# The dt columns of an input projection: from split operands on the whole array to unsplit operands in four column blocks

## The chip, the cores and the metric

The kernel runs on one core of one Trainium2 chip. The metric is the device time of one launch in microseconds (us), the median of several runs; lower is better. The profile is of a single execution on the same core. Its engines are TensorE (PE for matrix products, PEld for loading the stationary operand), VectorE (DVE), ScalarE (ACT), GpSimd (POOL) and SyncE (SP, which here only issues DMAs).

## What is computed

One step of a hybrid decoder layer for 320 tokens (256 of a prompt, 64 = 8 x 8 of a batch of samples), model width 2048, all in float32. Cut to what matters here:

```python
h = rms_norm(x, p["norm_mix_pre"])
proj = h @ p["w_in"]                       # 2048 x 9248
a_u, a_v, z, xbc, dt_raw = ...             # columns 0, 2048, 4096, 6144, 9216:9248
gate_out = chunk_spatial_gate(a_u, a_v, ...)
xbc = silu(causal_depthwise_conv(xbc, ...))
dt = softplus(dt_raw + dt_bias)            # 32 heads
y, new_state = ssd_scan(xs, dt, -exp(a_log), bm, cm, state)
x = x + rms_norm(concat(gate_out, gated_norm(y)) @ p["w_out"])
x = x + rms_norm(conv_ffn(rms_norm(x), ...))
```

The change concerns `dt_raw`: the last 32 columns of the input projection, one for each SSD head, for all 320 tokens.

## The kernel before

**Layout.** Activations stand with features on partitions: x is 16 tiles of 128 features by 320 tokens. The input norm is split in two: `x_ready` (L539 on) multiplies each tile by its norm weight (`pre`, 16 columns) and splits the product into a high part `h_hi` and a remainder `h_lo`, both of the type fp32r. The reciprocal root `r1` of the mean square, a number for each token, is made later (`with_r1`) and multiplied onto the results of a projection when they leave PSUM.

**A projection** (`project`, L154 on) streams weights in slabs of 512 KB through three buffers: SP loads `wraw`, ACT casts it to `whi` (L119), DVE makes the remainder `wlo` (L121). A block of 128 x 128 weights then costs three products of 128 x 320 (`accumulate`, L130 to L132: hi by hi, hi by lo, lo by hi). A slab has eight such blocks, 24 products. Four PSUM buffers (pool `mm`) hold the four output tiles of a projection, so the next one waits for a buffer until its evacuation is done. A second PSUM pool, `ms`, has four buffers for small things (`misc`).

**Order.** First v (`v_pass` 0 to 3), then B and C of the SSD part (`conv_proj`), then dt, then the first group of SSD heads (`heads_in(0)`), then u, the gate's product and the rest. A list of generators, `bg`, holds background work: `tick` advances its first generator by one step, and `project` ticks after most slabs. The Tile framework's scheduler places each instruction in its engine's queue by priority; each engine then runs its queue in order.

**The first 64 us.** `flat` is a view of the tile `vt`, which is later filled with v: until then it holds `pre` and the unnormalised x (`xf`). `with_r1` sits in `bg`: it waits seven ticks, sums the squares, runs three Newton steps on DVE (L230 to L236), then transposes the result over the partitions (`spread`, L272), copies it to `r1` (ACT, L274) and issues the DMAs of `params` (L328 on). `turned(0)` writes the first part of v into `vt` after the second `v_pass`.

**dt before** (`steps`, L421 on): two slabs of 8 x 128 columns are loaded, the last 128 columns of `w_in`, of which the last 32 are dt's. They go through the same cast, remainder and 48 products as any other (tile `ps_dt`, a buffer of `mm`); rows 96 to 127 of the result are used. DVE multiplies by `r1` (L430, tile `dtf`), POOL repeats the sample columns (L431, L433), and later five transposes (L438, tile `dt_ps`) bring dt to tokens on partitions. From there come the softplus, the cumulated sums and the decays.

Of the kernel before, what the change touches and what calls it, by code (L numbers as in the profile page):

```python
# [9 lines left out]
F32 = mybir.dt.float32  # L10
# [3 lines left out]
ALU = mybir.AluOpType  # L14
# [3 lines left out]
P = 128  # L18
NP = 256
NB, TS = 8, 8  # L20
NS = NB * TS
NT = NP + NS
D = 2048
KD = D // P
DFF = 5632
NF = DFF // P
NH = 32
# [3 lines left out]
U0, V0, Z0, X0, B0, C0, DT0 = 0, 2048, 4096, 6144, 8192, 8704, 9216  # L31
# [3 lines left out]
def hybrid_step(  # L35
# [10 lines left out]
    act, dve, pool, pe, sp = nc.scalar, nc.vector, nc.gpsimd, nc.tensor, nc.sync  # L46

    w_in, w_out, ffn_w_up, ffn_w_down = w_in[0], w_out[0], ffn_w_up[0], ffn_w_down[0]
# [5 lines left out]
    mm = ctx.enter_context(tc.tile_pool(name="mm", bufs=4, space=PSUM))  # L54
    ms = ctx.enter_context(tc.tile_pool(name="ms", bufs=4, space=PSUM))

    def misc(name):
        return ms.tile([P, 512], F32, tag="ms", name=name)


    ident = cp.tile([P, P], F32, name="ident")
# [3 lines left out]
    with tc.high_priority(offset=300000):  # L65
        dve.memset(ones, 1.0)

        ps = misc("early")
# [10 lines left out]
    def masks():  # L79
        make_upper_triangular(nc, upper, 1.0, diag=True)  # L80
        make_lower_triangular(nc, later, 1.0, diag=False)
        make_block_diagonal(nc, bd2, TS)

        for r in range(4):
            rs = slice(32 * r, 32 * r + 32)
            pool.tensor_copy(bsel[rs], bd2[rs, rs].rearrange("p (b t) -> p b t", b=4)[:, :, 0])
        for r in range(2):
            rs = slice(64 * r, 64 * r + 64)
            dve.tensor_tensor(out=upper_s[rs], in0=upper[rs, rs], in1=bd2[rs, rs], op=ALU.mult)
        pool.memset(cmask, 1.0)  # L90
        cm4 = cmask.rearrange("p (h b) i -> p h b i", h=2)
        pool.affine_select(out=cm4, in_=cm4, pattern=[[0, 2], [-8, 4], [1, 32]],
                           compare_op=ALU.is_ge, fill=0.0, base=0, channel_multiplier=0)
        pool.affine_select(out=cm4, in_=cm4, pattern=[[0, 2], [8, 4], [-1, 32]],
                           compare_op=ALU.is_ge, fill=0.0, base=7, channel_multiplier=0)
# [8 lines left out]
    def first():  # L104

        return tc.high_priority(offset=200000)
# [5 lines left out]
    def slab(src):  # L112
        n = src.shape[2]
        with tc.high_priority(offset=100000):
            m = n * src.shape[1]
            raw = first_raw.pop(0) if first_raw else wp.tile([P, 1024], F32, tag="wraw", name="wraw", bufs=3)
            slab_load.append(sp.dma_start(raw[:, :m].rearrange("p (a n) -> p a n", n=n), src).ins)
            hi = wp.tile([P, 1024], F32R, tag="whi", name="whi", bufs=3)
            act.copy(hi[:, :m], raw[:, :m])  # L119
            lo = wp.tile([P, 1024], F32R, tag="wlo", name="wlo", bufs=3)  # L120
            dve.tensor_tensor(out=lo[:, :m], in0=raw[:, :m], in1=hi[:, :m].bitcast(F32), op=ALU.subtract)  # L121

        def block(k, c):
            o = k * n + c * P
            return hi[:, o:o + P], lo[:, o:o + P]
        return block

    def accumulate(ps, w, xhi, xlo, first, last):
        whi, wlo = w
        pe.matmul(ps, whi, xhi, start=first, stop=False)  # L130
        pe.matmul(ps, whi, xlo, start=False, stop=False)  # L131
        return pe.matmul(ps, wlo, xhi, start=False, stop=last).ins  # L132

    def rows_of(w, k0, nk, c0, n):
        return w[k0 * P:(k0 + nk) * P, c0:c0 + n].rearrange("(k p) n -> p k n", p=P)

    hT = [None, None]


    bg = []  # L140
# [84 lines left out]
    def rsqrt_of(ss, scale, n, rows=P):  # L225

        v = tp.tile([P, n], F32, tag=f"rs_v{n}", name="rs_v")[:rows]
        r = tp.tile([P, n], F32, tag=f"rs_r{n}", name="rs_r", bufs=3)[:rows]
        t = tp.tile([P, n], F32, tag=f"rs_t{n}", name="rs_t")[:rows]
        dve.tensor_scalar(out=v, in0=ss, scalar1=scale, scalar2=EPS, op0=ALU.mult, op1=ALU.add)  # L230
        dve.tensor_scalar(out=r.bitcast(I32), in0=v.bitcast(I32), scalar1=-0.5, scalar2=float(0x5F3759DF),
                          op0=ALU.mult, op1=ALU.add)
        for _ in range(3):
            dve.scalar_tensor_tensor(out=t, in0=v, scalar=-0.5, in1=r, op0=ALU.mult, op1=ALU.mult)
            dve.tensor_tensor(out=t, in0=t, in1=r, op=ALU.mult)
            ins = dve.scalar_tensor_tensor(out=r, in0=t, scalar=1.5, in1=r, op0=ALU.add, op1=ALU.mult).ins  # L236
        rsqrt_ins.append(ins)
        return r
# [20 lines left out]
    def token_sums(sq, ps=None, more=False):  # L259

        begins = ps is None
        ps = misc("tsum") if begins else ps
        for c, o in enumerate((0, P, NT - P)):
            ins = pe.matmul(ps[:, c:c + 1], sq[:, o:o + P], ones[:, 0:1], start=begins and c == 0, stop=not more and c == 2).ins  # L264
        sums_ins.append(ins)
        return ps if more else ps[:, 0:3]

    def spread(r, out=None):

        ps = misc("spread")  # L270
        for c, o in ((2, NT - P), (0, 0), (1, P)):
            spread_ins.append(pe.transpose(ps[:, o:o + P], r[:, c:c + 1].to_broadcast([P, P]), ident).ins)  # L272
        if out is not None:
            act.copy(out, ps[:, :NT])  # L274
        return ps[:, :NT]
# [43 lines left out]
    r1 = hp.tile([P, NT], F32, name="r1")  # L319
# [51 lines left out]
    with ExitStack() as mctx:  # L371
        op = mctx.enter_context(tc.tile_pool(name="op", bufs=1))
# [3 lines left out]
        LP = 347  # L376
# [41 lines left out]
        dec = op.tile([P, 5, NH], F32, name="dec")  # L418
        ed = op.tile([P, 4, 4], F32, name="ed")

        def steps():  # L421

            ps_dt = mm.tile([P, 512], F32, tag="mm", name="ps_dt")
            for s in range(2):
                wb = slab(rows_of(w_in, 8 * s, 8, DT0 - 96, P))
                for k in range(8):
                    kt = 8 * s + k
                    accumulate(ps_dt[:, :NT], wb(k, 0), hT[0][:, kt, :], hT[1][:, kt, :], kt == 0, kt == KD - 1)
            dtf = op.tile([P, NT + NS + 2 * P], F32, tag="dtf", name="dtf", bufs=1)
            dve.tensor_tensor(out=dtf[96:, :NT], in0=ps_dt[96:, :NT], in1=r1[96:], op=ALU.mult)  # L430
            pool.tensor_copy(dtf[96:, NT:NT + NS], dtf[96:, NP:NT])  # L431
            for i in range(2):
                pool.tensor_copy(dtf[96:, (3 + i) * P:(4 + i) * P].rearrange("p (q t) -> p q t", q=4),  # L433
                                 dtf[96:, NP + 32 * i:NP + 32 * i + 32].unsqueeze(1).to_broadcast([32, 4, 32]))
            yield
            ps = misc("dt_ps")
            for c in range(5):
                pe.transpose(ps[:, NH * c:NH * c + NH], dtf[96:, P * c:P * c + P], ident[96:, 96:])  # L438
            H5 = 5 * NH
            dve.tensor_tensor(out=dt, in0=ps[:, :H5].rearrange("p (c h) -> p c h", c=5),  # L440
                              in1=bias_bc.unsqueeze(1).to_broadcast([P, 5, NH]), op=ALU.add)

            e = op.tile([P, 5, NH], F32, name="sp_e")
            q = dec
# [22 lines left out]
            ps = misc("cs_ps")  # L467
# [15 lines left out]
            ps = misc("csT_ps")  # L483
# [12 lines left out]
            ps = misc("dec_ps")  # L496
# [4 lines left out]
            for r in range(2):  # L501
                rs = slice(32 * r, 32 * r + 32)
                pool.tensor_tensor(out=later_s[:, r], in0=later[:NS, rs].unsqueeze(1).to_broadcast([NS, 4, 32]),
                                   in1=bd[:, rs].unsqueeze(1).to_broadcast([NS, 4, 32]), op=ALU.mult)
                pe.matmul(ps[:, (3 + r) * NH:(4 + r) * NH], later_s[:, r].rearrange("p q t -> p (q t)"), da[:NS, 2],
                          start=True, stop=True)
# [10 lines left out]
        with tc.tile_pool(name="gp", bufs=1) as gp:  # L517
# [4 lines left out]
            pre = flat[:, :KD]  # L522
            xf = flat[:, KD:KD + KD * NT].rearrange("p (k n) -> p k n", n=NT)
            masks()

            wS = gp.tile([P, 4, NB, TS], F32, name="wS")
            pool.memset(wS[NS:], 0.0)
# [38 lines left out]
            def with_r1():  # L566
                yield from repeat(None, 7)
                with first():
                    dve.tensor_tensor(out=acc[:, 0, :], in0=acc[:, 0, :], in1=acc[:, 1, :], op=ALU.add)
                    r = rsqrt_of(token_sums(acc[:, 0, :]), 1.0 / D, 3)  # L570
                yield
                spread(r, r1)
                params()
                yield

            after_v = []

# [96 lines left out]
                    if j % 2:  # L674
                        yield

            spare_pads = op.tile([P, 4, NT], F32, tag="xs", name="xs_pads", bufs=2).rearrange("p k n -> p (k n)")
            spare_pads = [spare_pads[:, LP * i:LP * i + LP] for i in range(3)]
            normed = layer_norm()
            bg.append(normed)  # L680
            conv_proj(B0, 16, lambda j: bT[:, j, :], 50000)
            behind(bT[:, 0, 0:1])
            conv_proj(C0, 20, lambda j: cT[:, j, :], 50000)
            tasks = steps()
            next(tasks)
            bg.append(tasks)
            x0 = heads_in(0)
            finish(normed)
            uf = gate_up(0)
# [12 lines left out]
        with tc.tile_pool(name="sd", bufs=1) as sd:  # L702
# [8 lines left out]
            for c in range(4):  # L711
                ps = misc("bt_ps")
# [185 lines left out]
            tasks = [ssd(g) for g in range(4)]  # L898
# [114 lines left out]
    with tc.tile_pool(name="fp", bufs=1) as fp:  # L1013
# [190 lines left out]
        for ks in [slice(k, k + 2) for k in range(0, 10, 2)] + [slice(10, 11)]:  # L1204
            f = acc[:, ks, :]
            n = ks.stop - ks.start
# [5 lines left out]
        for ks in (slice(11, 12), slice(12, 14), slice(14, 16)):  # L1212
            f = acc[:, ks, :]
            n = ks.stop - ks.start
# [87 lines left out]
```

## Time and profile before

| | us |
|---|---|
| median of 3 runs | 1789.76 (1789.74 to 1791.35) |
| the profiled execution, its own time | 1790.97 |
| span of that execution, first to last instruction | 1789.3 |

The granted TensorE clock in the profile is 0.998 of full speed. In the timelines below, the columns are start in us, duration in us, engine, line, operation, output and inputs, partitions by columns of the stationary operand, shape of what is written or streamed, number of merged instructions, and in brackets the engine's idle time before it with what ended it. A matrix product's shown duration includes the time until its last result is out; products overlap, so what one costs the array is the distance from its start to the next start. In views of groups, the two numbers after the bar are busy us and the mean of one in ns. An fp32 product stands in the trace as two instructions (64 calls at L812 give 128 records), an fp32r product as one.

### The profile page before, as it was taken

The numbers are of one execution on the slowest core, as the hardware profiler recorded it, in microseconds if no ns is written. First come the engines' busy times: TensorE is split into PE (matmuls) and PEld (weight loads), VectorE is DVE, ScalarE is ACT, GpSimd is POOL, SyncE is SP. The second block draws the span as 40 slices with busy tenths as digits, with TensorE's granted clock in tenths as the row PEclk, the third lists the DMA queues.
The fourth block names the chain that finished last, engine by engine and source line by source line (L and its number), as shares of the span: only waits on it lengthen the run. The fifth ranks groups of instructions, "written<-read, shape, count | busy, mean of one in ns | idle before, by whom it ended". The sixth has DMA issues, their size and how long they took to land.

```text
span 1789.3 us, 31254 instructions
## 1 busy us (share of the span) xinstructions
PE 1775.5 (99%) x12241; PEld 1744.7 (98%) x12241; DVE 1191.2 (67%) x2058; ACT 794.3 (44%) x1101; POOL 276.6 (15%) x591
## 2 busy tenths in 40 slices
PE   9999999999999999999999999999999999999998
PEld 9999999999999898999999999999999999999997
DVE  7448664557867778577866675767666575656565
ACT  6343455333535364445645434443434343433334
POOL 2003200000210111002322212121101020101004
PEclk9999999999999999999999999999999999999999
DMA  7455544445664644454565656566554444444442
GB/s 246 144 165 165 189 148 153 153 153 179 226 198 147 201 154 151 142 170 153 161 196 191 206 181 202 182 197 206 183 185 154 153 147 153 156 149 149 154 156 95
DMA packets 228082, 303.83 MB, mean 170 GB/s; under 512 B 17408, under 2 KB 149856, under 8 KB 227744
## 3 DMA queue, kind: packets, MB, share of 16 engines
q1 hardware_dynamic: 216288, 281.89, 49.4%
q10 hardware_dynamic: 10160, 15.47, 2.4%
q0 software_dynamic: 1488, 4.49, 0.8%
q8 instruction: 96, 1.57, 0.4%
q14 instruction: 50, 0.41, 0.1%
HBM read 284.23 MB, written 17.58 MB: 169 GB/s over the span
## 4 chain that ended last, share of the span: by engine, by line
PE 92%; DVE 4%; DMA 1%; issue 1%; ACT 1%; POOL 0%; SPq 0%; DVEq 0%; ACTq 0%; POOLq 0%
PE ps L130 19%; PE ps L132 19%; PE ps L131 19%; PE pd L130 10%; PE pd L132 10%; PE pd L131 10%; DVE wlo L121 1%; PE y_ps L859 1%; PE yo_ps L812 1%; PE tsum L264 0%; PE sg L663 0%; PE up_ps L1152 0%; DMA wraw<-in_w_in 0%; DVE acc_mix L998 0%; PE xt_ps L360 0%
## 5 line engine op out<-in xcount | busy, mean ns | idle before, releaser
L121 DVE TENSOR_TENSOR wlo<-wraw,whi 128x1024 fp32r<-128x1024 f32 x472 | 588.7, 1248 | 385.3 <-ACT whi L119 382.6
L119 ACT CAST whi<-wraw 128x1024 fp32r<-128x1024 f32 x472 | 494.2, 1047 | 726.1 <-PE ps L131 430.7
L130 PE MATMUL ps<-h_hi,whi 128*128 128x320 f32 x2528 | 784.5, 311 | 2.8 <-DVE dtf L430 2.1
L131 PE MATMUL ps<-h_lo,whi 128*128 128x320 f32 x2528 | 780.4, 309 | 0.0
L132 PE MATMUL ps<-h_hi,wlo 128*128 128x320 f32 x2528 | 779.4, 309 | 0.5 <-DVE wlo L121 0.2
L130 PEld LDWEIGHTS ps<-h_hi,whi 128*128 128x128 f32 x2528 | 474.6, 188 | 8.4 <-issue 3.8
L131 PEld LDWEIGHTS ps<-h_lo,whi 128*128 128x128 f32 x2528 | 474.8, 188 | 1.5 <-issue 0.5
L132 PEld LDWEIGHTS ps<-h_hi,wlo 128*128 128x128 f32 x2528 | 474.1, 188 | 2.0 <-DVE wlo L121 1.8
L130 PE MATMUL pd<-fhi,whi 128*128 128x320 f32 x704 | 217.3, 309 | 0.0
L132 PE MATMUL pd<-fhi,wlo 128*128 128x320 f32 x704 | 217.3, 309 | 0.0
L131 PE MATMUL pd<-flo,whi 128*128 128x320 f32 x704 | 217.3, 309 | 0.0
L130 PE MATMUL pd<-ohi,whi 128*128 128x320 f32 x448 | 140.8, 314 | 0.0
L131 PE MATMUL pd<-olo,whi 128*128 128x320 f32 x448 | 139.2, 311 | 0.0
L132 PE MATMUL pd<-ohi,wlo 128*128 128x320 f32 x448 | 138.9, 310 | 0.0
L131 PEld LDWEIGHTS pd<-flo,whi 128*128 128x128 f32 x704 | 132.2, 188 | 0.7
L132 PEld LDWEIGHTS pd<-fhi,wlo 128*128 128x128 f32 x704 | 132.2, 188 | 0.0
L130 PEld LDWEIGHTS pd<-fhi,whi 128*128 128x128 f32 x704 | 132.2, 188 | 0.0
L216 DVE TENSOR_TENSOR acc_ffn<-acc_ffn,pd 128x320 f32<-128x320 f32 x160 | 77.5, 484 | 35.8 <-PE pd L132 34.8
L130 PEld LDWEIGHTS pd<-ohi,whi 128*128 128x128 f32 x448 | 84.1, 188 | 4.0 <-issue 2.5
L132 PEld LDWEIGHTS pd<-ohi,wlo 128*128 128x128 f32 x448 | 84.1, 188 | 0.6 <-issue 0.6
L131 PEld LDWEIGHTS pd<-olo,whi 128*128 128x128 f32 x448 | 84.2, 188 | 0.2 <-issue 0.2
L1049 POOL COPY ptf<-pad 128x2 f32<-128x2 f32 x88 | 20.8, 238 | 406.5 <-DVE pad L1037 406.0
(297 smaller groups left out, 1588.1 us busy)
## 6 DMA issues: line engine op xcount, KB each, us to landing
wraw<-in_ffn_w_up SPq DMA_DIRECT2D x176, 512.0 KB, 3.5
wraw<-in_w_in SPq DMA_DIRECT2D x144, 512.0 KB, 3.5
wraw<-in_ffn_w_down SPq DMA_DIRECT2D x88, 512.0 KB, 3.3
wraw<-in_w_out SPq DMA_DIRECT2D x64, 512.0 KB, 3.3
st<-in_state_ssm SPq DMA_DIRECT2D x64, 256.0 KB, 3.8
out_ssm_state_sample<-st ACTq DMA_DIRECT2D x32, 256.0 KB, 2.7
cs<-dacs_d SPq DMA_DIRECT2D x16, 320.0 KB, 3.5
xr<-in_xT SPq DMA_DIRECT2D x4, 640.0 KB, 4.6
```

Source lines behind the costliest of these rows:

```text
L119: act.copy(hi[:, :m], raw[:, :m])
L121: dve.tensor_tensor(out=lo[:, :m], in0=raw[:, :m], in1=hi[:, :m].bitcast(F32), op=ALU.subtract)
L130: pe.matmul(ps, whi, xhi, start=first, stop=False)
L131: pe.matmul(ps, whi, xlo, start=False, stop=False)
L132: return pe.matmul(ps, wlo, xhi, start=False, stop=last).ins
L216: dve.tensor_tensor(out=acc[:, nb, :], in0=acc[:, nb, :], in1=ps[:, :NT], op=ALU.add)
L812: pe.matmul(ps_yo[row:row + 32, :256], cms[:, 4 * h + i, :], st[h][:, 256 * r:256 * r + 256], start=i == 0, stop=i == 3, tile_position=(0, ...
L859: pe.matmul(ps[64 * i:64 * i + 64, cols], w(hl), x(hl, m, cpx), tile_position=(0, 64 * i), **flags)
L1049: pool.tensor_copy(ptf[:, k, :], pad[:, 256:258])
```

## The change

- dt's products leave `steps`. A new generator `dt_columns`, started in `with_r1` behind `params()`, loads the 32 columns alone into the tile `dt_w` (128 x 16 x 32, 256 KB in runs of 128 bytes) on SP's queue. POOL multiplies them by `pre`.
- Seven ticks later, 16 fp32 products of 128 x 32 weights by 128 x 320 of the unsplit `xf` follow. Feature tiles 4i to 4i+3 go to the column blocks 0, 32, 64 and 96 of the array, and so to four quarters of the partitions of one PSUM tile (`dt_four`, a `misc` buffer): each quarter sums four of the 16 feature tiles.
- DVE evacuates all four quarters in one instruction with `r1`; POOL's three copies now cover 128 partitions.
- The five transposes become five fp32 products with `heads4`, a 128 x 32 matrix with four ones in each column, which adds the four quarters while it transposes. `heads4` is made at the start by three additions on DVE, in the unused end of the tile `xs_pads`, which is allocated earlier for that.
- The scheduler's order changes in few other places. On PE, the `tsum` products of `with_r1` stand behind 156 of the first pass's 192 weight products (153 before), `spread` behind 184 (175 before), and the dt products behind 96 of the second pass's 192. On DVE, two of `heads4`'s additions stand ahead of `rs_v`, and the remainder of the second pass's second slab (L121) stands ahead of the last Newton instruction instead of behind it. On SP, the 276 KB load `prm` stands one slab later, and `dt_w` stands behind the slab that was issued at 31.59 us. On POOL, the clearing of a part of `vt` stands behind the multiplication of `dt_w`.

```diff
+        def dt_columns(xf, pre):
+
+            w = op.tile([P, NT + NS + 2 * P], F32, tag="dtf", name="dt_w", bufs=1)[:, :KD * NH].rearrange("p (k n) -> p k n", n=NH)
+            sp.dma_start(w, rows_of(w_in, 0, KD, DT0, NH))
+            pool.tensor_tensor(out=w, in0=w, in1=pre.unsqueeze(2).to_broadcast([P, KD, NH]), op=ALU.mult)
+            yield from repeat(None, 7)
+            ps = misc("dt_four")
+            for i in range(4):
+                for q in range(4):
+                    at = slice(NH * q, NH * q + NH)
+                    pe.matmul(ps[at, :NT], w[:, 4 * i + q, :], xf[:, 4 * i + q, :], start=i == 0, stop=i == 3, tile_position=(0, NH * q))
+            dtf = op.tile([P, NT + NS + 2 * P], F32, tag="dtf", name="dtf", bufs=1)
+            dve.tensor_tensor(out=dtf[:, :NT], in0=ps[:, :NT], in1=r1, op=ALU.mult)
+            dt_parts.append(dtf)
+            yield
+            pool.tensor_copy(dtf[:, NT:NT + NS], dtf[:, NP:NT])
+            for i in range(2):
+                pool.tensor_copy(dtf[:, (3 + i) * P:(4 + i) * P].rearrange("p (q t) -> p q t", q=4),
+                                 dtf[:, NP + 32 * i:NP + 32 * i + 32].unsqueeze(1).to_broadcast([P, 4, 32]))
...
         def steps():
 
-            ps_dt = mm.tile([P, 512], F32, tag="mm", name="ps_dt")
-            for s in range(2):
-                wb = slab(rows_of(w_in, 8 * s, 8, DT0 - 96, P))
-                for k in range(8):
-                    kt = 8 * s + k
-                    accumulate(ps_dt[:, :NT], wb(k, 0), hT[0][:, kt, :], hT[1][:, kt, :], kt == 0, kt == KD - 1)
-            dtf = op.tile([P, NT + NS + 2 * P], F32, tag="dtf", name="dtf", bufs=1)
-            dve.tensor_tensor(out=dtf[96:, :NT], in0=ps_dt[96:, :NT], in1=r1[96:], op=ALU.mult)
...
-            yield
+            dtf = dt_parts[0]
             ps = misc("dt_ps")
             for c in range(5):
-                pe.transpose(ps[:, NH * c:NH * c + NH], dtf[96:, P * c:P * c + P], ident[96:, 96:])
+                pe.matmul(ps[:, NH * c:NH * c + NH], dtf[:, P * c:P * c + P], heads4, start=True, stop=True)
...
+            heads4 = spare_xs[:, 4 * NT - NH:]
+            dve.tensor_tensor(out=heads4, in0=ident[:, :NH], in1=ident[:, NH:2 * NH], op=ALU.add)
+            for q in (2, 3):
+                dve.tensor_tensor(out=heads4, in0=heads4, in1=ident[:, NH * q:NH * q + NH], op=ALU.add)
...
                 spread(r, r1)
                 params()
-                yield
+                dt_task = dt_columns(xf, pre)
+                next(dt_task)
+                bg.append(dt_task)
...
-            tasks = steps()
-            next(tasks)
-            bg.append(tasks)
+            bg.append(steps())
```

More of the change, by code (lines that the diff above doesn't have):

```diff
@@ L419, in hybrid_step @@
         ed = op.tile([P, 4, 4], F32, name="ed")
-        def steps():
-            ps_dt = mm.tile([P, 512], F32, tag="mm", name="ps_dt")
-            for s in range(2):
-                wb = slab(rows_of(w_in, 8 * s, 8, DT0 - 96, P))
-                for k in range(8):
-                    kt = 8 * s + k
-                    accumulate(ps_dt[:, :NT], wb(k, 0), hT[0][:, kt, :], hT[1][:, kt, :], kt == 0, kt == KD - 1)
-            dtf = op.tile([P, NT + NS + 2 * P], F32, tag="dtf", name="dtf", bufs=1)
[L430 to L434, printed above, removed]
-            yield
+        dt_parts = []
@@ L524, in hybrid_step @@
             masks()
+            spare_xs = op.tile([P, 4, NT], F32, tag="xs", name="xs_pads", bufs=2).rearrange("p k n -> p (k n)")
+            spare_pads = [spare_xs[:, LP * i:LP * i + LP] for i in range(3)]
+            heads4 = spare_xs[:, 4 * NT - NH:]
+            dve.tensor_tensor(out=heads4, in0=ident[:, :NH], in1=ident[:, NH:2 * NH], op=ALU.add)
+            for q in (2, 3):
+                dve.tensor_tensor(out=heads4, in0=heads4, in1=ident[:, NH * q:NH * q + NH], op=ALU.add)
             wS = gp.tile([P, 4, NB, TS], F32, name="wS")
@@ L675, in gate_mix @@
                         yield
-            spare_pads = op.tile([P, 4, NT], F32, tag="xs", name="xs_pads", bufs=2).rearrange("p k n -> p (k n)")
-            spare_pads = [spare_pads[:, LP * i:LP * i + LP] for i in range(3)]
             normed = layer_norm()
```

## The prediction

> **What bounds the kernel now.** I read the page first, then the groups by line and shape, then the tiles that the change touches, and last the timelines around them. The page:
>
> ```profile
> span 1789.3 us, 31254 instructions
> PE 1775.5 (99%) x12241; PEld 1744.7 (98%) x12241; DVE 1191.2 (67%) x2058; ACT 794.3 (44%) x1101; POOL 276.6 (15%) x591
> PE 92%; DVE 4%; DMA 1%; issue 1%; ACT 1%; POOL 0%; SPq 0%; DVEq 0%; ACTq 0%; POOLq 0%
> ```
>
> PE is never idle for long and carries 92% of the chain that ended last. So a change is worth the array time that it takes out of PE's queue, plus the waits that it removes, less what it adds. The tile `ps_dt`:
>
> ```profile
> L130 PE MATMUL ps_dt<-h_hi,whi x16: 310/310/310, 183.0 to 189.6; 128*128 128x320 f32 x16
> L132 PE MATMUL ps_dt<-h_hi,wlo x16: 310/310/310, 183.3 to 189.9; 128*128 128x320 f32 x16
>   PE ps L130: 2.1, 1
> ```
>
> The 16 triples run from 183.0 to 189.6: 6.6/15 = 0.44 us each, 0.147 a product, whatever the 310 ns of one with its latency. The last row is a waiter: PE stood 2.1 us for the evacuation of this tile. PE's timeline around it:
>
> ```profile
> 192.54 0.31 PE L132 MATMUL ps<-h_hi,wlo 128*128 128x320 f32 x1
> 194.93 0.41 PE L130 MATMUL ps<-h_hi,whi 128*128 128x320 f32 x1 [2.08 <-DVE dtf L430]
> 195.18 0.31 PE L131 MATMUL ps<-h_lo,whi 128*128 128x320 f32 x1
> ```
>
> `ps_dt` took the buffer that the fourth tile of `heads_in(0)` needs. From start to start the wait costs 194.93 - 192.54 - 0.147 = 2.24, and 0.10 more at the next, slower start (0.25 for 0.147): 2.35 us.
>
> **Removed: the products, -7.04.** 48 x 0.1467 = 7.04 us. The two slabs' loads, casts and remainders go too, but PE's pace of 24 x 0.147 = 3.52 us a slab set their rhythm, so they are worth nothing of their own.
>
> **Removed: the wait, -2.05.** With `ps_dt` gone, `heads_in(0)` starts where it stood, in the time frame of before at 183.0, and its slabs take over dt's places in the three buffers. Is something else late then?
>
> ```profile
> 185.33 0.21 DVE L393 TENSOR_TENSOR pad<-ps,r 128x64 f32<-128x64 f32 x1
> 191.54 1.23 DVE wlo L121
> 195.89 1.31 DVE L121 TENSOR_TENSOR wlo<-wraw,whi 128x1024 fp32r<-128x1024 f32 x1
> ```
>
> The fourth buffer is free at 185.54 and wanted after 18 products, at 185.65: just in time. The fourth slab's remainder is there at 192.8 (its load was slow, but that belongs to its place in time), and its first use is at 183.0 + 3 x 3.52 + 0.29 = 193.9: fine. The fifth is wanted at 197.4 and was there at 197.2; in the new order six operations of the convolution stand ahead of it where there were five and L430, about as long. I take 0.3 us of a new wait there. Bounds: the whole wait gone (2.35), or all of it back under another name (0).
>
> **Added: the 16 dt products, +2.5.** The trace of before has the same weight shape in four column blocks at L812 (128*32, fp32, 256 columns streamed), and two blocks at L859:
>
> ```profile
> 452.00 0.31 PE L132 MATMUL ps<-h_hi,wlo 128*128 128x320 f32 x1
> 452.24 0.64 PE L812 MATMUL yo_ps<-st,cb_cms 128*32 128x256 f32 x8
> 452.81 0.41 PE L130 MATMUL ps<-h_hi,whi 128*128 128x320 f32 x1
> 453.06 0.31 PE L131 MATMUL ps<-h_lo,whi 128*128 128x320 f32 x1
> L812 PE MATMUL yo_ps<-st,cb_cms 128*32 128x256 f32 x128 | 10.2, 391 | 0.0
> ...
> 488.61 0.39 PE L859 MATMUL y_ps<-cpx,s 128*64 128x128 f32 x4
> 488.83 0.28 PE L859 MATMUL y_ps<-cs,xdt 128*64 128x64 f32 x4
> ```
>
> Eight instructions of 391 ns lie within 0.64 us: 0.64 - 0.39 = 0.25 from the first start to the last, so four run side by side, then the other four. At L859 two rounds of 128 columns take 488.83 - 488.61 = 0.22, 0.11 a round, and they follow each other with no loss though they accumulate into the same place. A round of 320 columns is then 0.11 x 2.5 = 0.27; by the first two rounds of L812 it would be 0.24 x 320/256 = 0.30. dt has 32 instructions in eight rounds: 2.2 us (up to 2.4). Going into column blocks and back costs what L812 shows: 453.06 - 452.00 - 2 x 0.147 = 0.77 for two rounds of 0.24, so 0.29. Sum 2.45 to 2.7; I take 2.5.
>
> The Trainium skill speaks for less overlap: "TensorE: Matmul & The Clock Gate", Part 3, gives three column tiles a measured 2.38 times, not 3. An estimate from that page: four tiles at the same share give 3.2 times, 32 x 0.27 / 3.2 = 2.7 us, and the sum would be 0.2 higher. L812's eight instructions in 0.64 us leave no room for such a loss, so the rows decide.
>
> **Added: dt to tokens, +0.45.** Five transposes become five fp32 products with 128-column weights, ten instructions. The nearest row is `tsum`, fp32 with 128-column weights and little to stream:
>
> ```profile
> 220.41 0.31 PE L132 MATMUL ps<-h_hi,wlo 128*128 128x320 f32 x1
> 221.33 0.31 PE L131 MATMUL ps<-h_lo,whi 128*128 128x320 f32 x1
> ...
> 29.15 0.31 PE L132 MATMUL ps<-h_hi,wlo 128*128 128x320 f32 x1
> 29.30 0.73 PE L264 MATMUL tsum<-ones,acc_mix 128*128 128x1 f32 x6
> 29.89 0.39 PE L130 MATMUL ps<-h_hi,whi 128*128 128x320 f32 x1
> 30.12 0.31 PE L131 MATMUL ps<-h_lo,whi 128*128 128x320 f32 x1
> ```
>
> The transposes cost 221.33 - 220.41 - 0.29 = 0.63. Six `tsum` instructions cost 30.12 - 29.15 - 0.29 = 0.68, (29.89 - 29.30)/6 = 0.10 each; four more make 1.08. Difference 0.45.
>
> **Moved: the chain to `r1`, +0.2.** The first pass's evacuations wait for `r1`, and the second pass needs their buffers.
>
> ```profile
> 33.05 0.16 DVE L236 SCALAR_TENSOR_TENSOR rs_r<-rs_t,rs_r 128x3 f32<-128x3 f32 x1
> 33.31 1.23 DVE L121 TENSOR_TENSOR wlo<-wraw,whi 128x1024 fp32r<-128x1024 f32 x1
> 34.45 1.28 DVE L339 TENSOR_TENSOR ev<-ps,r 128x320 f32<-128x320 f32 x3
> ...
> 33.35 0.51 PE L272 MATMUL spread<-ident,rs_r 128*128 128x128 f32 x3
> 33.62 0.40 PE L131 MATMUL ps<-h_lo,whi 128*128 128x320 f32 x1
> 33.90 0.43 ACT L274 COPY r<-spread 128x320 f32<-128x320 f32 x1
> ...
> 21.55 0.31 PE L131 MATMUL ps<-h_lo,whi 128*128 128x320 f32 x1
> 22.01 0.42 PE L132 MATMUL ps<-h_hi,wlo 128*128 128x320 f32 x1
> ```
>
> In the new order DVE does two short additions (some 0.16 each, as 33.05) for `heads4` ahead of `rs_v`, and a remainder (1.2 us) ahead of the last Newton instruction: `rs_r` ends near 34.8, not 33.2. Queued behind it on PE are `spread` and the pass's last eight products. PE now reaches `spread` nine products later, at 34.65, so it stands some 0.2 us. The second pass starts at 36.4 instead of 36.2; `r1` is copied by 35.85 and the first buffer free at 36.35, just in time. Bounds: -0.4 (at 22.01 PE waited 0.3, and 0.1 in the next start, for a remainder that comes earlier in the new order) to +1.2 (PE stands the full lateness of `r1`).
>
> **Free edits.** The narrow load of 2048 runs:
>
> ```profile
> bias_bc<-in_ssm_dt_bias SPq DMA_DIRECT2D x1, 16.0 KB, 4.1
> st<-in_state_ssm SPq DMA_DIRECT2D x64, 256.0 KB, 3.8
> 31.59 7.41 SPq L117 DMA_DIRECT2D wraw<-in_w_in  x3
> L788 POOL TENSOR_TENSOR xde<-xdt,dec 128x512 f32<-128x512 f32 x8 | 10.6, 1323 | 92.9 <-ACT bsp L719 51.1 <-PE s_ps L801 15.2 <-DVE xdt L752 14.1
> 43.34 1.05 ACT L119 CAST whi<-wraw 128x1024 fp32r<-128x1024 f32 x1 [2.47 <-PE ps L131]
> ```
>
> It is issued behind the slab of 31.59, at 32.0, lands some 4 us later (the same bytes took 3.8, runs of 128 bytes 4.1), and POOL needs 1.3: ready at 37.5. PE asks 96 products after 36.2, at 50.3, so 13 us cover it. Without that cover each us late is a us of PE, with all later weights queued behind. The slabs behind the load on SP have cover too: ACT's cast at 43.34 waited for PE (a free `whi`), not for its load. `prm` is first read by the convolutions, far later. DVE's 0.5 us evacuation and POOL's copies have until 220 us. `vt`'s clearing and filling wait for the dt products, which stand 96 products ahead of `turned(0)`.
>
> **Sum.** -7.04 - 2.05 + 2.5 + 0.45 + 0.2 = -5.9 us. The profiled execution's own time, 1790.97, is 1.7 above its span and 1.2 above the median of the runs shown; it would become 1785.1. Against the median: 1789.76 - 5.9 = 1783.9.
>
> **Rivals.**
> (1) The wait stays: DVE's backlog, not the buffer, is what PE meets at 183 to 198. For it: the chain of waits runs through DVE's `wlo` there. Against: the margins above, 0.1 us and 1.1 us. 1783.9 + 2.05 = 1786.0.
> (2) The blocks stream one after another, the change not doing what it says: 32 x 0.27 = 8.7 for 2.2, so 1790.4. Against: L812.
> (3) Slower: the column blocks not only run singly but each instruction drains and loads anew. For it: four different x tiles stream at once, which L812 does with two tiles only.
>
> ```profile
> L1182 PE MATMUL x1p<-acc_mix,ident 128*128 128x320 f32 x22 | 7.4, 454 | 2.4 <-DVE acc_ffn L1210 2.4
> L812 PEld LDWEIGHTS yo_ps<-st,cb_cms x128: 106/108/109, 452.2 to 703.1; 128*32 128x32 f32 x128
> ```
>
> A full fp32 product of 320 columns is 0.454, a load 0.108: 32 x 0.56 = 18.0 for 2.5, so 1799.4. It decides once an instruction costs over 0.26 (8.4 in all): from there the sum is positive.
> (4) The narrow load is late. It costs nothing until it takes over 17 us (50.3 - 32.0 - 1.3). At the rate of `bias_bc`, 128 runs in 4.1, it would be 66 us and the kernel 49 slower, 1833; but 4.1 is hardly above the 3.5 to 3.8 of wide loads, so it is latency, not runs. The Trainium skill, "DMA: Bandwidth & Descriptors", Specifications, asks for 512 bytes or more a transfer and warns of a read-modify-write below; no run here shows yet what that does to 2048 runs.
>
> **Chances.** Forecast 0.76, (1) 0.12, (2) 0.04, (3) 0.04, (4) 0.02, other 0.02. About 0.2%, 3.6 us, is what a measurement of this kernel tells from none: the line is at 1786.2. The forecast and half of (1) are faster: 0.80; half of (1), (2) and half of the rest same: 0.14; (3), (4) and the rest slower: 0.06. The forecast with its bounds (wait 0.3 lower; chain 0.6 lower or 1.0 higher; dt products up to 0.2 higher) spans 1782.9 to 1785.1; with (1) and something for stretches that I did not follow, 1781.5 to 1787.5.
>
> **What would show it.** `dt_four`: 32 records within about 2.5 us near 50 us, PE not idle before them. No wait of over 0.5 us on PE near the start of `heads_in(0)`. `spread` about 1.5 us later than 33.35 with PE idle under 0.5 before it. `dt_ps` about 1.1 us of PE. Wrong would be starts of `dt_four` 0.27 apart one by one, PE waiting for `dt_w`, or DVE's `wlo` as releaser near 186 to 198.

## The result and the profile after

| | before | after |
|---|---|---|
| median of 7 runs, us | 1789.74 (1789.29 to 1791.77) | 1784.25 (1783.26 to 1785.42) |
| ratio | | 0.9969 (95%: 0.9959 to 0.9978) |
| the profiled execution, own time and span | 1790.97, 1789.3 | 1783.26, 1781.5 |

The kernel is 5.5 us faster; the forecast was 5.9 (1783.9). The two spans differ by 7.8, more than the medians: the profiled execution of before is one of its longer ones, that of after its shortest. A second profiled execution of each was therefore taken (below, "before again", 1788.84, and "after again", 1783.49).

The page of after, its span, engines and chain of waits:

```profile
span 1781.5 us, 31219 instructions
PE 1770.1 (99%) x12230; PEld 1739.0 (98%) x12230; DVE 1189.2 (67%) x2059; ACT 792.3 (44%) x1099; POOL 275.9 (15%) x592
PE 95%; DVE 3%; ACT 1%; issue 1%; DMA 1%; SPq 0%; DVEq 0%; ACTq 0%
```

PE is still busy for 99% of the span, and its share of the chain has risen from 92% to 95%. The new products, in PE's timeline of after:

```profile
49.86 0.31 PE L132 MATMUL ps<-h_hi,wlo 128*128 128x320 f32 x1
50.10 2.36 PE L433 MATMUL dt_four<-vt,dt_w 128*32 128x320 f32 x32
52.39 0.41 PE L130 MATMUL ps<-h_hi,whi 128*128 128x320 f32 x1
52.65 0.31 PE L131 MATMUL ps<-h_lo,whi 128*128 128x320 f32 x1
```

All 32 instructions lie within 2.36 us, and no idle time stands before them. They cost 52.65 - 49.86 - 2 x 0.147 = 2.50 us. In the view of the tile `dt_four` one instruction lasts 432 ns and the first and last start are 50.1 and 52.0: eight rounds of four, (52.0 - 50.1)/7 = 0.27 apart.

PE where `heads_in(0)` now wants its fourth buffer, in the timeline of after:

```profile
186.96 0.31 PE L132 MATMUL ps<-h_hi,wlo 128*128 128x320 f32 x1
187.11 0.31 PE L130 MATMUL ps<-h_hi,whi 128*128 128x320 f32 x1
187.26 0.31 PE L131 MATMUL ps<-h_lo,whi 128*128 128x320 f32 x1
```

Here before stood for 2.08 us; after goes on at 0.147 a product. The chain to `r1` (PE, DVE, ACT, POOL and SP rows of the timeline of after):

```profile
31.68 0.46 SPq L426 DMA_DIRECT2D dt_w<-in_w_in  x1
...
32.83 1.23 DVE L121 TENSOR_TENSOR wlo<-wraw,whi 128x1024 fp32r<-128x1024 f32 x1
33.63 0.31 PE L130 MATMUL ps<-h_hi,whi 128*128 128x320 f32 x1
33.97 0.15 DVE L236 SCALAR_TENSOR_TENSOR rs_r<-rs_t,rs_r 128x3 f32<-128x3 f32 x1
34.27 0.51 PE L272 MATMUL spread<-ident,rs_r 128*128 128x128 f32 x3 [0.33 <-DVE rs_r L236]
34.82 0.43 ACT L274 COPY r<-spread 128x320 f32<-128x320 f32 x1 [1.75 <-PE spread L272]
35.28 1.69 DVE L339 TENSOR_TENSOR ev<-ps,r 128x320 f32<-128x320 f32 x4 [1.15 <-ACT r L274]
35.83 0.41 PE L130 MATMUL ps<-h_hi,whi 128*128 128x320 f32 x1
36.69 1.05 POOL L427 TENSOR_TENSOR dt_w<-dt_w,vt 128x512 f32<-128x512 f32 x1 [7.27 <-DVE ev L339]
```

PE waits 0.33 us for the last Newton instruction, which now has a remainder (32.83) ahead of it; in after again this wait is 0.17. The narrow load is asked for at 31.68 and has landed by 36.69, where POOL starts; the products come 12.4 us after POOL has ended.

**Where the time went.** Each weight product of before has its counterpart in after. The distance between the two starts, followed along PE's queue, changes only where one kernel gains or loses. Places are times of before. The columns compare the first profiled executions and the second ones (us, worked out from the starts):

```
                                    forecast   first pair   second pair
to 35 us, with the chain to r1       +0.2        -0.27        +0.22
the dt products                      +2.5        +2.49        +2.49
short stops at 157, 176 and 180       -          -0.76         0
the 48 products of ps_dt             -7.04       -7.04        -7.05
the wait for dtf                     -2.05       -2.35        -1.19
dt to tokens                         +0.45       +0.49        +0.49
the rest, with the end                -          -0.30        -0.33
span                                 -5.9        -7.74        -5.37
```

The array's own terms are the same in both pairs to 0.01. What differs are waits: before's own wait for `dtf` was 2.35 us in one execution and 1.19 in the other. Most of what stands in the first row arose ahead of 15 us, before the chain to `r1` begins: -0.34 and +0.30. From there on the row is worth +0.07 and -0.08.

### The profile page after: what moved, and what is told of

Same layout as the page of the kernel before. It is cut to its first block, busy times and chain, and to the rows that moved or that the text cites. A ratio compares the mean times of both kernels' runs of the same rounds, so it can differ in the third digit from the quotient of the medians.

```text
span 1781.5 us, 31219 instructions
## 1 busy us (share of the span) xinstructions
PE 1770.1 (99%) x12230; PEld 1739.0 (98%) x12230; DVE 1189.2 (67%) x2059; ACT 792.3 (44%) x1099; POOL 275.9 (15%) x592
## 4 chain that ended last, share of the span: by engine, by line
PE 95%; DVE 3%; ACT 1%; issue 1%; DMA 1%; SPq 0%; DVEq 0%; ACTq 0%
PE ps L130 20%; PE ps L132 20%; PE ps L131 20%; PE pd L130 10%; PE pd L132 10%; PE pd L131 10%; PE y_ps L873 1%; DVE wlo L121 1%; PE yo_ps L826 1%; PE sg L681 0%; PE up_ps L1166 0%; PE tsum L264 0%; DVE acc_mix L1012 0%; PE xt_ps L360 0%; ACT whi L119 0%
## 5 line engine op out<-in xcount | busy, mean ns | idle before, releaser
L121 DVE TENSOR_TENSOR wlo<-wraw,whi 128x1024 fp32r<-128x1024 f32 x470 | 584.6, 1244 | 380.0 <-ACT whi L119 377.2
```

## The experiments

### Before again, and after again

Both kernels unchanged, a second profile of each.

> The kernel before once more, to see what two profiles of one program differ by. Theory (the waits of 0.1 to 0.3 us near 157, 176 and 180 us, and steps of some 0.1 to 0.5 us between 640 and 860 us, come and go from run to run): some of these differ from the first profile of before, span within 0.6 of 1789.3. Rival (these waits belong to the program): the same waits to 0.05 us.

> The changed kernel once more, on the same chip as the version with transposes. Theory: span 1781.2 to 1782.2, the dt products 2.5 us again, no wait at the start of heads_in(0); time 5 to 6.5 us under before.

Measured: 1788.84 (one run) and 1784.0 (median of 5; 1783.33 to 1785.56), beside 1790.15 (median of 9; 1788.96 to 1791.01) for before on the same chip: 0.9967 (0.9955 to 0.998). The 5.5 us of the first measurement return as 6.15. The expectation for before missed: its span is 1787.1, 2.2 below the first, where 0.6 was allowed. That for after held, with a span of 1781.8. PE's timeline of before again, at the wait for `dtf`:

```profile
191.40 0.31 PE L132 MATMUL ps<-h_hi,wlo 128*128 128x320 f32 x1
192.63 0.41 PE L130 MATMUL ps<-h_hi,whi 128*128 128x320 f32 x1 [0.92 <-DVE dtf L430]
192.88 0.31 PE L131 MATMUL ps<-h_lo,whi 128*128 128x320 f32 x1
```

The wait is 192.88 - 191.40 - 2 x 0.147 = 1.19 us here, half of the first. Why, ACT and DVE show, first in the first execution of before:

```profile
190.45 1.05 ACT L119 CAST whi<-wraw 128x1024 fp32r<-128x1024 f32 x1 [3.18 <-DMA wraw<-in_w_in]
...
191.54 1.23 DVE L121 TENSOR_TENSOR wlo<-wraw,whi 128x1024 fp32r<-128x1024 f32 x1 [1.06 <-ACT whi L119]
...
194.38 0.50 DVE L430 TENSOR_TENSOR dtf<-ps_dt,r 32x320 f32<-32x320 f32 x1
```

and then in before again:

```profile
187.91 1.05 ACT L119 CAST whi<-wraw 128x1024 fp32r<-128x1024 f32 x1 [1.80 <-DMA wraw<-in_w_in]
...
189.24 1.22 DVE L121 TENSOR_TENSOR wlo<-wraw,whi 128x1024 fp32r<-128x1024 f32 x1
...
192.07 0.50 DVE L430 TENSOR_TENSOR dtf<-ps_dt,r 32x320 f32<-32x320 f32 x1
```

L430 is queued on DVE behind the fourth slab's remainder, which needs that slab's cast, which waits for its load. Measured from the first `ps_dt` product (183.0 and 181.9), the cast began at 7.5 us in the first execution and at 6.0 in the second. In the first, DVE stood 1.06 us for the cast; in the second it came to the remainder without idle time, and L430 started 10.2 us after the first product in place of 11.4. So the difference between the two waits comes from the landing of a load, and the 1.19 us of the second are what is left when DVE's queue alone is late. The prediction read one execution as if it were the kernel's.

### dt's old products in a buffer of the other pool

Before, with the accumulator out of the pool `mm`; nothing else moves on any engine.

```diff
-            ps_dt = mm.tile([P, 512], F32, tag="mm", name="ps_dt")
+            ps_dt = misc("ps_dt")
```

> The kernel before, with the dt tile taken from the pool of small PSUM tiles instead of the pool of the projections; nothing else moves. Theory (the wait is for the buffer): PE's 2.08 us wait on dtf is gone, 2.0 to 2.35 us come off, span about 1787.0 instead of 1789.3, and no wait of over 0.5 us stands between 183 and 200 us. Rival (DVE's backlog is what PE meets): PE waits about as long, now for a remainder (wlo), span 1789.3.

Measured: 1788.73 (median of 11) beside 1790.16 (27 runs): 0.9995 (0.9986 to 1.0004), span 1786.6. PE's busy time in one window, with its start and end, length, PE busy, instructions, granted clock, DMA share and GB/s, in the first execution of before:

```profile
150.00:200.00 50.00, 47.85 (x322) 1.00 0.60 191
```

before again:

```profile
150.00:200.00 50.00, 49.08 (x335) 1.00 0.62 200
```

and this kernel:

```profile
150.00:200.00 50.00, 50.00 (x340) 1.00 0.61 193
```

No idle time is left, though all 48 products are still there and L430 is no earlier: it started 10.4 us after the first of them (193.0 and 182.6 in the view of the tile), between the 10.2 and 11.4 of the two executions of before. The wait was the buffer and nothing else: rival 1, that DVE's backlog would stop PE under another name, falls for this stretch. In the median it is worth 1.4 us, at the lower end of the two waits, and its interval holds zero; the time alone would not have shown it.

### The second half of the kernel 2.5 us later

Does a later start alone change the waits of 157 to 198 us? Before, with 17 products of the high part of x with itself in the second pass, where the dt products stand in after; their result is not read.

```diff
-                yield
+                yield from repeat(None, 7)
+                ps = misc("spent")
+                for k in range(17):
+                    pe.matmul(ps[:, :NT], hT[0][:, k % KD, :P], hT[0][:, k % KD, :], start=True, stop=True)
```

> The kernel before with 17 further fp32r products of 128 x 320 in PE's queue in the second pass of v, results unread: 17 x 0.147 = 2.49 us, as much as the new dt products took. Theory (the stretch from 140 to 195 us is set by DVE and its loads, so a PE that comes later waits less there): the waits near 157, 176 and 180 us (0.76 in all) go and the wait for dtf shrinks from 2.2 to about 1.5, so the span grows by 1.0 to 1.3 only, to 1790.3 to 1790.6. Rival (those 0.76 us came from the change's own order or from less DVE work): it grows by the full 2.5, to 1791.8.

Measured: 1792.12 (10 runs) beside 1790.16: 1.0011 (1.0002 to 1.002), span 1791.5. The products cost 2.48. PE's timeline of this kernel:

```profile
159.73 0.38 PE L130 MATMUL ps<-h_hi,whi 128*128 128x320 f32 x1 [0.32 <-DVE xs_pads L393]
...
195.06 0.31 PE L132 MATMUL ps<-h_hi,wlo 128*128 128x320 f32 x1
196.61 0.41 PE L130 MATMUL ps<-h_hi,whi 128*128 128x320 f32 x1 [1.24 <-DVE dtf L430]
196.87 0.31 PE L131 MATMUL ps<-h_lo,whi 128*128 128x320 f32 x1
```

The wait is 196.87 - 195.06 - 0.294 = 1.52: below the first execution's 2.35, above the second's 1.19, and a new stop of 0.32 has come at 159.73. The span of 1791.5 lies near the rival's 1791.8 and not at the theory's 1790.3 to 1790.6. But waits vary by about as much between two executions of before, so one execution does not tell whether a later start shortens them; the question stays open.

### All sixteen products in one column block

After, with every feature tile in block 0 and the other three quarters of `dtf` set to zero, so that the sum is the same.

```diff
-                    at = slice(NH * q, NH * q + NH)
-                    pe.matmul(ps[at, :NT], w[:, 4 * i + q, :], xf[:, 4 * i + q, :], start=i == 0, stop=i == 3, tile_position=(0, NH * q))
+                    k = 4 * i + q
+                    pe.matmul(ps[:NH, :NT], w[:, k, :], xf[:, k, :], start=k == 0, stop=k == KD - 1, tile_position=(0, 0))
...
+            pool.memset(dtf[NH:64], 0.0)
+            pool.memset(dtf[64:], 0.0)
...
```

> The changed kernel with all 16 dt products in one column block, summed into one quarter of the partitions; the other quarters are set to zero. Theory (four blocks stream side by side, one streams 32 instructions in turn at 0.27 us with its weight loads hidden): the dt products take 8.6 to 8.9 us instead of 2.5, span 1781.5 + 6.3 = 1787.8, still below the 1789.3 of before. Rival (each instruction also pays its weight load or a drain): 14 to 18 us, span 1793 to 1797. Rival (blocks bring nothing): 1781.5.

Measured: 1790.09 (10 runs) beside 1790.16: 1.0002 (0.9993 to 1.0011), span 1787.6. PE's timeline of this kernel:

```profile
49.74 0.31 PE L132 MATMUL ps<-h_hi,wlo 128*128 128x320 f32 x1
49.98 8.80 PE L433 MATMUL dt_four<-vt,dt_w 128*32 128x320 f32 x32
58.71 0.41 PE L130 MATMUL ps<-h_hi,whi 128*128 128x320 f32 x1
58.96 0.31 PE L131 MATMUL ps<-h_lo,whi 128*128 128x320 f32 x1
```

58.96 - 49.74 - 0.294 = 8.93 us in place of 2.50. Side by side is worth 6.4 us, and that is the whole gain: unsplit operands alone cost the array more than the 48 split products that they replace (7.04), and only the wait removed with these makes up for it. The prediction's rival 2 put this case at 1790.4. Per streaming round, 32 in the place of eight are four times; the Trainium skill ("TensorE: Matmul & The Clock Gate", Part 3) measured 2.38 times for three column tiles. No run here has three; for four, the same share would be an estimated 3.2 times, and these runs show more: 8.93 to 2.50 is 3.6 times even with the fixed cost of about 0.3 us at the entry and the end included.

### Block by block in place of round by round

After, with the two loops exchanged: each block's four products stand together in the program. The order on the other engines is that of after.

```diff
-            for i in range(4):
-                for q in range(4):
+            for q in range(4):
+                for i in range(4):
```

> The changed kernel with the loops over blocks and feature tiles exchanged: each column block gets its four products (eight instructions) in a row, then the next. Theory (PE starts products in the queue's order, so only neighbours in the queue lie side by side): 32 instructions in 29 rounds of 0.27 us, 7.8 us, dt products 8.1 us with going in and out, span 1781.5 + 5.6 = 1787.1. Rival (the blocks run on independently of the order): 2.5 us, span 1781.5.

Measured: 1786.35 (one run), span 1784.7. PE's timeline of this kernel:

```profile
49.89 0.31 PE L132 MATMUL ps<-h_hi,wlo 128*128 128x320 f32 x1
50.13 5.66 PE L433 MATMUL dt_four<-vt,dt_w 128*32 128x320 f32 x32
55.72 0.41 PE L130 MATMUL ps<-h_hi,whi 128*128 128x320 f32 x1
55.97 0.31 PE L131 MATMUL ps<-h_lo,whi 128*128 128x320 f32 x1
```

55.97 - 49.89 - 0.294 = 5.79 us, 3.3 more than after: neither the one number that was expected nor the other. The starts say why:

```
50.126 50.419 50.688 50.958 | 51.227 51.233  51.496 51.526  51.765 51.795  ...  54.248 54.278 | 54.547 54.816 55.085 55.354
```

Four instructions start alone, then come twelve pairs, then four alone: 20 rounds of 0.27. In one block only one instruction streams at a time (the experiment before), so a pair is two blocks, and the next block has begun when the last one is at its fifth instruction of eight. The durations bear this out. All other instructions last 432 or 433 ns in the trace, but the first one of a block lasts 457: in after the four that start first, in the one-block kernel the first alone, and here the ones that start at 50.126, 51.233, 52.339 and 53.446, four rounds apart. So the order costs PE 3.3 us, but not all of the gain is lost with it: the time of this one run is still 3.8 us below the 1790.15 of before.

### The products asked for early

After, with one step of waiting in place of seven, to see the edge of the narrow load's cover.

```diff
-            yield from repeat(None, 7)
+            yield from repeat(None, 1)
```

> The changed kernel with the dt products one tick behind their load instead of seven: they then stand behind 10 of the second pass's products on PE, at about 37.3 us, where in the changed kernel POOL had the weights ready at 37.74. Theory (nothing else covers the load): PE stands 0.3 to 0.7 us ahead of the products with POOL's product as releaser, and the span grows by as much, 1781.8 to 1782.2. Rival (the load's 128-byte runs take longer when they are asked for beside the first slabs): PE stands over 2 us, span over 1783.5.

Measured: 1783.73 (one run), span 1782.0. PE and POOL in the timeline of this kernel:

```profile
36.35 1.05 POOL L427 TENSOR_TENSOR dt_w<-dt_w,vt 128x512 f32<-128x512 f32 x1 [6.97 <-DVE ev L339]
...
37.03 0.31 PE L130 MATMUL ps<-h_hi,whi 128*128 128x320 f32 x1
37.46 2.36 PE L433 MATMUL dt_four<-vt,dt_w 128*32 128x320 f32 x32
39.75 0.41 PE L131 MATMUL ps<-h_lo,whi 128*128 128x320 f32 x1
```

POOL is done at 37.40 and PE starts at 37.46, only 37.46 - 37.03 - 0.147 = 0.28 late, of which after shows 0.09 (50.10 - 49.86 - 0.147) with everything ready. So 0.19 us are due to the early start, and the 12 us of cover that after gives the weights are hardly needed. The span is 0.5 above that of after, as was forecast, but by luck: followed along PE's queue, most of it came from short stops at 178 to 187 us (0.53).

### Transposes and additions in place of the matrix of ones

After, without `heads4`: five transposes of 128 x 128 bring all four quarters to tokens, and DVE adds them.

```diff
-            for c in range(5):
-                pe.matmul(ps[:, NH * c:NH * c + NH], dtf[:, P * c:P * c + P], heads4, start=True, stop=True)
...
+            for c0, n in ((0, 4), (4, 1)):
+                ps = misc("dt_ps")
+                for c in range(n):
+                    pe.transpose(ps[:, P * c:P * c + P], dtf[:, P * (c0 + c):P * (c0 + c) + P], ident)
+                four = ps[:, :P * n].rearrange("p (c q h) -> p c q h", q=4, h=NH)
+                for q in range(4):
+                    dve.tensor_tensor(out=dt[:, c0:c0 + n], in0=four[:, :, q],
+                                      in1=dt[:, c0:c0 + n] if q else bias_bc.unsqueeze(1).to_broadcast([P, n, NH]), op=ALU.add)
...
```

> The changed kernel without heads4: five transposes of 128 x 128 again, and DVE adds the four quarters. Theory: the transposes cost PE about 0.65 us instead of 1.1, and without heads4's additions the scheduler puts the remainder behind the last Newton step again, so PE does not stand 0.33 us ahead of spread: 0.4 to 0.9 us less, span 1780.6 to 1781.1. Rival (the chain to r1 costs nothing in the changed kernel): only the 0.45 of the transposes, 1781.1; rival (DVE's eight additions lie on the path): 1781.5 or more.

> The changed kernel without heads4, with five transposes and DVE's additions, once more beside the changed kernel. Theory: 0.45 to 0.57 us less at the transposes and 0.2 to 0.3 less before the second pass, so 0.3 to 0.9 us less than the changed kernel in the span, and its time below that of the changed kernel by no more than that. Rival: the 1.7 us between the medians seen so far are real.

Measured: 1782.52 (5 runs; 1782.14 to 1782.97), ratio 0.996 (0.9947 to 0.9972); again, beside after again, 1782.83 (5 runs; 1782.57 to 1783.64), 0.996 (0.9947 to 0.9974). PE's timeline of after at these products:

```profile
212.48 0.31 PE L132 MATMUL ps<-h_hi,wlo 128*128 128x320 f32 x1
212.63 1.20 PE L448 MATMUL dt_ps<-xs_pads,dtf 128*128 128x32 f32 x10
213.66 0.40 PE L130 MATMUL ps<-h_hi,whi 128*128 128x320 f32 x1
213.89 0.31 PE L131 MATMUL ps<-h_lo,whi 128*128 128x320 f32 x1
```

and of this kernel:

```profile
212.65 0.31 PE L132 MATMUL ps<-h_hi,wlo 128*128 128x320 f32 x1
212.79 0.71 PE L450 MATMUL dt_ps<-ident,dtf 128*128 128x128 f32 x5
213.26 0.39 PE L130 MATMUL ps<-h_hi,whi 128*128 128x320 f32 x1
213.49 0.30 PE L131 MATMUL ps<-h_lo,whi 128*128 128x320 f32 x1
```

213.89 - 212.48 - 0.294 = 1.12 us against 213.49 - 212.65 - 0.294 = 0.55: five instructions instead of ten save 0.57 on PE, and of seven more additions on DVE PE meets no more than 0.08, near 238 us. In neither execution does PE wait ahead of `spread`. This is the fastest version seen: its ten runs lie between 1782.14 and 1783.64, the twelve of after between 1783.26 and 1785.56. The 0.57 is shown. The medians differ by 1.2 to 1.7, more than the 0.3 to 0.9 that was expected, and the rest isn't settled. The spans of the two pairs of profiles differ by only -0.3 and +0.15, with short stops coming and going at 176 to 187 and near 640 us; but of this kernel the profiled executions are the longest of their five runs, and of after the shortest and the second shortest. The scheduler also placed some other instructions on PE, DVE, ACT and SP otherwise than in after, which was not tested by itself.

## Why the prediction came out right

- **The bound.** PE's queue decided, and terms added up along it: the table above accounts for the span of either pair.
- **Products removed, -7.04.** -7.04 and -7.05. The slabs' casts and remainders that went with them were indeed worth nothing: in the buffer experiment they are still there and PE does not stop.
- **dt products, +2.5.** 2.49. The price came from another tile with two rounds; with eight rounds and four different x tiles it held. Rivals 2 and 3 (1790.4 and 1799.4) fall: the one-block kernel is what rival 2 would have been, and an instruction there costs 0.27, not 0.56.
- **dt to tokens, +0.45.** 0.49.
- **The chain to `r1`, +0.2.** The wait was named rightly: PE stands for `rs_r` at `spread`, 0.33 and 0.17 us in the two executions, against the 0.2 worked out. The time was off: `rs_r` ended at 34.12 where 34.8 was worked out, and `spread` started 0.9 us later than before, not 1.5. The two additions of `heads4` delayed nothing, since DVE still stood 0.87 us for `tsum` behind them, and this execution of after was 0.3 us ahead from its start. The whole stretch gave -0.27 in one pair and +0.22 in the other, both within the bounds; the part of it behind 15 us gave +0.07 and -0.08, so the term was nearer to nothing than to 0.2.
- **The wait for `dtf`, -2.05.** Right in mechanism, mis-sized twice. No new wait came, so the 0.3 kept back for one was not needed. And the 2.35 it was kept back from was one execution's figure: 1.19 in the other, 1.52 with a later start. The step that failed is the sentence that a slow load "belongs to its place in time": it set the wait's size, through ACT's cast and DVE's queue. The two errors have opposite signs; that the term came out between the two measured waits is in part luck. With the predicted other terms (-7.04 + 2.5 + 0.45 + 0.2 = -3.89) and no new wait, 1.19 and 2.35 give sums of -5.1 and -6.2; measured were -5.5 and -6.15.
- **What was not in the sum:** three short stops of 0.76 us in the first execution of before, absent from the second, and 0.3 at the end.
- **Chances.** By the prediction's own shares, the forecast and half of (1) are 0.82, not 0.80, and the other two sums 0.11 and 0.07, not 0.14 and 0.06. Nothing above hangs on it.
- **Rival 4, the narrow load.** POOL was ready at 37.74 in after and at 37.40 in the early kernel; 37.5 was the estimate. The view of DMA traffic of after, from 31 to 37 us in 40 slices of 0.15 us:

```profile
GB/s 347 283 206 121 115 64 37 29 89 137 109 41 150 273 355 341 369 410 396 423 330 225 217 218 216 218 216 218 219 145 99 232 123 218 246 369 355 369 355 396
wraw<-in_w_in SPq DMA_DIRECT2D x2, 512.0 KB, 4.6
dt_w<-in_w_in SPq DMA_DIRECT2D x1, 256.0 KB, 4.9
```

The load took 4.9 us from issue to landing, the slabs of twice the bytes 4.6. The runs of 128 bytes did cost something: while they moved alone (34.3 to 35.3 us) the rate was 216 to 219 GB/s; ahead of them, with a slab moving, it was up to 423. So "latency, not runs" was half of the matter, and the cover hid both.

## What to carry to other kernels

Narrow unsplit products paid here only because they were spread over the column blocks and stood in the program round by round: in one block all of the gain was lost, block by block 3.3 us of it on PE. Count what a change does to PE start to start against rows of the same kind: those terms held within 0.05 us. Waits do not: take a second profiled execution of the kernel before a wait of one or two us goes into a sum, and follow it to the load behind it.

## What the runs showed that was not expected

With the products of a block standing together, PE still ran two blocks at a time. In the program's queue the sixteen products stand strictly block by block; the scheduler did not mix them. Yet the first instruction of the second block started at 51.233, with five of the first block's eight started: it passed three that were queued ahead of it. The records do not name the block, so this is inferred from the starts (20 rounds where strict order gives 29 and free choice eight) and from the four that last 457 ns. Between column blocks, then, PE did not keep to the order of its queue. The Trainium skill ("TensorE: Matmul & The Clock Gate", Part 3, under what overlaps and what doesn't) says that products start and end in the order of the program, "strict FIFO, no reordering"; the starts of this run do not fit that.

The other surprise is how far the waits of one kernel move between executions: 0.92 and 2.08 us of idle time for the same instruction, while the terms of the array's products agree to 0.01 us.
